# Moving GpSimd's share of the feed-forward stages of a hybrid encoder trunk onto VectorE

## The chip, the core and the metric

The kernel runs on one core of a Trainium2 chip. The metric is the device time of one execution in microseconds; the median of three runs of the kernel before is 2620.11 us (2618.71 to 2625.42). TensorE is called PE in the profile (PEld is its weight load), VectorE DVE, ScalarE ACT, GpSimd POOL, and SP is the engine whose queue issues most DMAs. L1043 is line 1043 of the kernel.

## The reference, cut to what matters

Two layers run on 1040 rows (16 learned rows ahead of 1024 tokens) of width 1024, all in float32. Each layer is a mixer (delta-rule heads and a short gated convolution, with its input and output projections) and then a feed-forward block:

```
h = h + hybrid_mixer(rmsnorm(h, norm1_w[l]), ...) # ends in mix @ w_out
h = h + swiglu(rmsnorm(h, norm2_w[l]), w_gate_up[l], w_down[l])

def swiglu(h, w_gate_up, w_down):
    gate, up = jnp.split(h @ w_gate_up, 2, axis=-1)     # each 2816 wide = 22 tiles of 128
    return (jax.nn.silu(gate) * up) @ w_down
```

A last RMSNorm ends it. The change touches the second line of each layer, and the output projection that runs into it.

## The kernel before, in words

**Split products.** Every matrix product is made of three passes in a fast float32 format. A weight tile w is split into a high part `hi` (ScalarE copies w into the format, which rounds it) and a low part `lo = w - hi`; the activations are split likewise. TensorE then adds `hi*hi + hi*lo + lo*hi`. So each weight tile that arrives by DMA costs one ScalarE copy and one subtraction before its matmuls, and the subtraction is what this case is about. Five places make such weights or work beside them in the feed-forward stages:

- `wsplit` (L123 to L130), called by `wload` (L132) for ordinary projections. Its subtraction at L130 goes to VectorE where the flag `lov[0]` is true and to GpSimd otherwise. `lov[0]` is set by position in the mixer (L642 and L748); from the third mixer tile of the second loop on it is false, and it is set again at the start of the next layer (L642).
- `w_op` (L1038 to L1044), the weights of the gate and up products: copy at L1042, subtraction at L1043 on GpSimd. It writes into a ring of seven pairs of slots (`wslot`, L1028).
- `w_unit` (L1163 to L1182), the weights of the down product: copy at L1180, subtraction at L1181 on GpSimd.
- L1330, the scaling of the gate row `g` by the inverse norm `ss`, on GpSimd; L1331 scales the row `u` on VectorE, then ScalarE applies SiLU (L1332), VectorE multiplies (L1333), and the row goes to memory by DMA (L1334).
- L950 in `out_part`, the sum of squares of the new residual. It is on VectorE except for the even tiles of the second half (z = 1), which GpSimd adds.

**Stages of the feed-forward part, in order, in each layer.** *Output projection with norm*: `out_part(z, m)` finishes the mixer's output projection for each of eight row tiles m in two halves of the columns z, adds it to the residual (L905 on VectorE, reading PSUM), sums squares, and between those calls VectorE and ScalarE form the combinations B11, B21, T1, B22, T2, T3, T4 of the normed activations, high and low (L177, L965, L977, L1001). *Early gate/up*: two of seven products of the first four tiles. *Gate/up*: for each of 22 tiles f, four quarter weights arrive by DMA, VectorE forms four combinations (L1266, L1267, L1270, L1271), seven weights go through `w_op`, and seven products (Strassen's scheme with seven instead of eight) run on TensorE. Each product lands in a PSUM bank and is taken out by VectorE (L1289, L1300, L1303, L1307, L1316) or ScalarE (L1285, L1312) before the next product adds into the same bank: p5 is followed by p3 in one bank, p6 by p7 by p4 in another. In layer 1 a product is two groups (j = 0, 1) of 12 matmuls of 260 columns; in layer 2 one group of 12 of 512 columns. *Down*: 18 of the 22 tiles go through the same seven-product scheme in 84 units; `w_unit(u)` makes weights five units ahead, `t_pair(t)` reloads the gate/up results from memory and splits them (L1222 on ScalarE, L1223 on VectorE) into eight slots; results are taken out at L1406. The four remaining tiles are an ordinary product with `wload` (layer 1) or `last_weights` (layer 2, L1360). Layer 2 ends in the final RMSNorm, where L1425 alternates between VectorE and GpSimd.

**What sets the order.** Each engine runs its own instructions strictly in the order of its queue, and waits on semaphores for the others. The order is not written by hand: the framework takes instructions in order of a priority (program order, moved by `at_prio`) as a planned timeline makes them ready, and fixes one order for each engine when the kernel is built. So an instruction that changes its engine may shift the order of its neighbours.

Of the kernel before, what the change touches and what calls it, by code (L numbers as in the profile page):

```python
# [7 lines left out]
F32 = mybir.dt.float32  # L8
# [3 lines left out]
ALU = mybir.AluOpType  # L12
# [30 lines left out]
def trunk(ctx: ExitStack, tc: tile.TileContext, xT, w_in, w_ba, w_out, w_gu, w_dn,  # L43
# [8 lines left out]
    def nm(p):  # L52
        cnt[0] += 1
        return f"{p}_{cnt[0]}"
# [4 lines left out]
    def row(tag, dt=F32, bufs=1):  # L59
        return sb.tile([128, L], dt, tag=tag, bufs=bufs, name=nm(tag))  # L60
# [4 lines left out]
    def c4k(tag="c"):  # L65
        return sb.tile([128, L], F32, tag="c", bufs=2, name=nm(tag))
# [28 lines left out]
    def at_prio(p):  # L95
        tc.cur_priority = p
# [3 lines left out]
    tt = nc.vector.tensor_tensor  # L100
    stt = nc.vector.scalar_tensor_tensor
    ts = nc.vector.tensor_scalar
    ptt = nc.gpsimd.tensor_tensor
# [17 lines left out]
    lov = [False]  # L121
# [23 lines left out]
    def dense(ws, xs, chunks, evac, pool=None):  # L145

        for (n0, n1) in chunks:
            n = n1 - n0
            ps = (pool or pacc)()
            K = len(xs)  # L150
            here = tc.cur_priority
            if mmp[0] is not None:
                at_prio(mmp[0])
            for k in range(K):
                (wh, wl), (xh, xl) = ws[k], xs[k]
                mm(ps[:, :n], wh, xh[:, n0:n1], start=(k == 0), stop=False)  # L156
                mm(ps[:, :n], wh, xl[:, n0:n1], start=False, stop=False)  # L157
                mm(ps[:, :n], wl, xh[:, n0:n1], start=False, stop=(k == K - 1))  # L158
            if mmp[0] is not None:
                mmp[0] = tc.cur_priority  # L160
                at_prio(here)
            here = tc.cur_priority
            if evp[0] is not None:
                at_prio(evp[0])
            evac(ps[:, :n], n0, n1)
            if evp[0] is not None:
                evp[0] = tc.cur_priority
                at_prio(here)
            for q in (jobs, jobs2, jobs3):
                f = q.pop(0) if q else None  # L170
                if f is not None:
                    f()
# [106 lines left out]
    for l in range(DEPTH):  # L279
# [656 lines left out]
            return v[:, s, :] if len(ap.shape) == 2 else v[:, :, s, :]  # L936

        at_prio(base + 3000000)
        ss = row("rstd")

        def out_part(z, m):
            dense(wload(w_out[l, m, :, 0:4, :], 4), os_, hcut[z], add_h(m), pwide)

            v, sv = half(hr[m][:, o0:L], z), half(ss[:, o0:L], z)
            if m == 0:
                act(out=sv, in_=v, func=AF.Square)
            else:
                sq = c4k("sq")[:, 0:NB].rearrange("p (g e) -> p g e", g=2)
                act(out=sq, in_=v, func=AF.Square)
                (ptt if z == 1 and m % 2 == 0 else tt)(out=sv, in0=sv, in1=sq, op=ALU.add)  # L950
            for (n0, n1) in hcut[z]:
                dma(hd[m][:, n0:n1], hr[m][:, n0:n1])

# [84 lines left out]
        def w_op(src, early=False):  # L1038
            hi, lo = wslot(early)
            n = src.shape[1]  # L1040
            hi, lo = hi[:, 0:n, :], lo[:, 0:n, :]
            act(out=hi, in_=src, func=AF.Copy)  # L1042
            ptt(out=lo, in0=src, in1=hi.bitcast(F32), op=ALU.subtract)  # L1043
            return hi, lo  # L1044

        bn = [0]
# [32 lines left out]
        def pin(ps):  # L1079
            return loc(ps, 0)  # L1080
# [82 lines left out]
        def w_unit(u):  # L1163

            p, b, m = UNITS[u]
            n = 4 * b + m
            i = u % 8
            if i in (0, 4, 6):
                hi, lo = (wp.tile([128, WK, 128], F32R, tag=t, name=nm(t)).rearrange("p a b -> p (a b)")[:, 0:384] for t in ("whi", "wlo"))
            else:  # L1170
                j = {1: 0, 2: 1, 3: 2, 5: 3, 7: 4}[i]
                hi, lo = (dw["W"][:, 384 * (2 * j + q):384 * (2 * j + q) + 384] for q in range(2))
            if p in ("P5", "P6", "P7"):
                r = s_raw(n)
            elif p == "P3":
                r = a_raw(0, 1, n)
                tt(out=r, in0=r, in1=s_raw(n), op=ALU.subtract)
            else:
                r = a_raw(*{"P2": (0, 1), "P1": (0, 0), "P4": (1, 1)}[p], n)
            act(out=hi, in_=r, func=AF.Copy)  # L1180
            ptt(out=lo, in0=r, in1=hi.bitcast(F32), op=ALU.subtract)  # L1181
            dw["w", u] = [t.rearrange("p (k e) -> p k e", k=3) for t in (hi, lo)]  # L1182

        def t_raw(i):
# [71 lines left out]
        for f in range(FT):  # L1256
            A11, A12, A21, A22 = raw4("raw"), raw4("raw"), raw4("ck2"), raw4("ck2")
            dma(A11, w_gu[l, f, 0, :, 0:4, :])
            dma(A21, w_gu[l, f, 1, :, 0:4, :])
            dma(A22, w_gu[l, f, 1, :, 4:8, :])  # L1260
            dma(A12, w_gu[l, f, 0, :, 4:8, :])
            s1t, s2t = raw4("ck2"), raw4("ck2")
            W = {}
            if f >= NE:
                W["A11"] = w_op(A11)
            tt(out=s1t, in0=A21, in1=A22, op=ALU.add)  # L1266
            tt(out=s2t, in0=s1t, in1=A11, op=ALU.subtract)  # L1267
            W["S1"] = w_op(s1t)
            W["S2"] = w_op(s2t)
            tt(out=s2t, in0=A12, in1=s2t, op=ALU.subtract)  # L1270
            tt(out=A21, in0=A11, in1=A21, op=ALU.subtract)  # L1271
            end = f == FT - 1
            for n, a in ([("S3", A21), ("A22", A22), ("S4", s2t), ("A12", A12)] if end else
                         [("S4", s2t), ("S3", A21), ("A12", A12), ("A22", A22)]):
                if f >= NE or n != "A12":
                    W[n] = w_op(a)
            g, u = early[f] if f < NE else (row((X[1], Y[1])[f % 2] + "f"), row(X[1], F32, 3))
            ps = {}


            def p1(j):
                ps["a", j], ps["c", j], ps["b", j] = pbank(), pbank(), pbank()
                if f >= NE:
                    prod(ps["a", j], W["A11"], T["B11"], j, True)
                    act(out=part(u, 0, j), in_=pin(ps["a", j]), func=AF.Copy)  # L1285

            def p5(j):
                prod(ps["c", j], W["S1"], T["T1"], j, True)
                tt(out=part(u, 1, j), in0=pin(ps["c", j]), in1=part(u, 0, j), op=ALU.add)  # L1289

            def p3(j):
                prod(ps["c", j], W["S4"], T["B22"], j, False)
                (gadd if end else gset)(ps["c", j], j)

            def p6(j):
                prod(ps["b", j], W["S2"], T["T2"], j, True)
                (gset if end else gadd)(ps["b", j], j)

            def gset(p, j):
                tt(out=part(g, 1, j), in0=pin(p), in1=part(u, 0, j), op=ALU.add)  # L1300

            def gadd(p, j):
                tt(out=part(g, 1, j), in0=pin(p), in1=part(g, 1, j), op=ALU.add)  # L1303

            def p7(j):
                prod(ps["b", j], W["S3"], T["T3"], j, False)
                tt(out=part(u, 1, j), in0=pin(ps["b", j]), in1=part(u, 1, j), op=ALU.add)  # L1307

            def p2(j):
                if f >= NE:  # L1310
                    prod(ps["a", j], W["A12"], T["B21"], j, False)
                    act(out=part(g, 0, j), in_=pin(ps["a", j]), func=AF.Copy)  # L1312

            def p4(j):
                prod(ps["b", j], W["A22"], T["T4"], j, False)
                tt(out=part(u, 0, j), in0=pin(ps["b", j]), in1=part(u, 0, j), op=ALU.add)  # L1316

            p1_ = (p1, p6, p7)
            if end:

                for p in (p1, p5, p6, p7, p4, p3, p2):
                    for j in range(NJ):
                        p(j)
                    down_begins(p)
            else:
                for j in range(NJ):
                    for p in (p1, p5, p3, p6, p7, p2, p4):
                        p(j)
            gv, uv, rv = g[:, o0:L], u[:, o0:L], ss[:, o0:L]
            ptt(out=gv, in0=gv, in1=rv, op=ALU.mult)  # L1330
            tt(out=uv, in0=uv, in1=rv, op=ALU.mult)  # L1331
            act(out=gv, in_=gv, func=AF.Silu)  # L1332
            tt(out=uv, in0=uv, in1=gv, op=ALU.mult)  # L1333
            dma(ad[f][:, o0:L], uv)  # L1334
            if NF <= f < NF + NP:
                tt(out=gv[:, 0:NB].rearrange("p (g e) -> p g e", g=2), in0=half(uv, 1), in1=half(uv, 0), op=ALU.subtract)
                dma(td[f - NF], gv[:, 0:NB])
            s_under(f)
# [38 lines left out]
        for u, (p, b, m) in enumerate(UNITS):  # L1377
            if b == 1 and p in FIRST:
                dh, z = FIRST[p]
# [13 lines left out]
            for j in range(NJ):  # L1393
# [9 lines left out]
                if b == NBK - 1:  # L1403
                    dh, z, op = TO[p]
# [98 lines left out]
```

## Time and profile before

| what | value |
|---|---|
| median of the three timed runs | 2620.11 us |
| span of the profiled execution, first to last instruction | 2625.6 us |
| mean granted TensorE clock in it | 0.983 |
| PE busy | 2512.3 us, 17442 matmuls |
| DVE busy | 1650.8 us, 2481 instructions |
| ACT busy | 1046.0 us, 1933 instructions |
| POOL busy | 1105.2 us, 838 instructions |

The profile shows one execution; no time of its own beside its span is given, and the span is 5.5 us above the median of the timed runs. A busy time counts from the start to the end of each instruction, so time in which a started instruction is held up counts as busy. A wait is listed as the waiting engine and line, an arrow, and the instruction that came last before it could go on. Idle time of an engine that is not the bottleneck costs nothing.

### The profile page before, as it was taken

The page shows a single profiled execution, that of the slowest core. Times are in us where ns is not written, and L with a number is a line of the kernel's source. Part 1 is how long each engine was busy: PE and PEld are TensorE (multiplying, and loading weights), DVE is VectorE, ACT ScalarE, POOL GpSimd, SP SyncE. Part 2 cuts the span into 40 slices and gives each one's busy share as a digit, 9 for nine tenths or more (in the row PEclk, how much of TensorE's full clock was granted, in tenths as well). Part 3 has the DMA queues.
Part 4 walks back from the last instruction along what each step waited for, and adds up shares of the span by engine and source line. Part 5 has one row for each costly group of instructions (what it writes and reads, how often), then busy time and mean ns, then how long its engine had stood idle before and what let it go on. Part 6 is the DMA issues. An engine that isn't in the chain of part 4 may idle for free. (4 is left out here: it accounts for less than half of the span.)

```text
span 2625.6 us, 45152 instructions
## 1 busy us (share of the span) xinstructions
PE 2512.3 (96%) x17442; PEld 2292.3 (87%) x17442; DVE 1650.8 (63%) x2481; ACT 1046.0 (40%) x1933; POOL 1105.2 (42%) x838
## 2 busy tenths in 40 slices
PE   8999999998999999989999989999989999998997
PEld 6989999998899999989999878998967778886876
DVE  4678433648766666667656874235688777668656
ACT  5564332435233333434445633324442323333444
POOL 2041212225666666645321212222357666665552
PEclk9999999999999999989999989999999999999999
DMA  3458265524422222763224572545333232248431
GB/s 125 127 179 267 88 196 171 183 66 126 136 97 86 102 81 74 242 203 113 94 88 140 177 249 92 184 157 197 111 128 125 91 108 85 76 140 274 130 111 64
DMA packets 213571, 360.03 MB, mean 137 GB/s; under 512 B 25268, under 2 KB 87676, under 8 KB 213356
## 3 DMA queue, kind: packets, MB, share of 16 engines
q1 hardware_dynamic: 180684, 310.69, 36.1%
q10 hardware_dynamic: 30496, 42.09, 5.1%
q0 software_dynamic: 2176, 4.36, 0.6%
q8 instruction: 137, 2.24, 0.4%
q14 instruction: 78, 0.64, 0.1%
HBM read 266.60 MB, written 90.46 MB: 136 GB/s over the span
## 5 line engine op out<-in xcount | busy, mean ns | idle before, releaser
L130 POOL TENSOR_TENSOR wlo<-raw,whi 128x512 fp32r<-128x512 f32 x132 | 178.3, 1353 | 802.7 <-ACT whi L129 723.0
L156 PE MATMUL pacc<-a,whi 128*128 128x346 f32 (+1 forms) x808 | 265.3, 332 | 11.9 <-ACT whi L129 10.4
L158 PE MATMUL pacc<-a,wlo 128*128 128x346 f32 (+1 forms) x808 | 264.7, 329 | 1.4 <-DVE wlo L130 0.7
L156 PE MATMUL pacc<-b,whi 128*128 128x346 f32 (+2 forms) x672 | 235.7, 351 | 0.4 <-DVE a L730 0.4
L158 PE MATMUL pacc<-b,wlo 128*128 128x346 f32 (+2 forms) x672 | 232.7, 348 | 0.0
L157 PE MATMUL pacc<-a,whi 128*128 128x346 f32 (+1 forms) x688 | 226.9, 330 | 2.6 <-DVE a L900 2.4
L157 PE MATMUL pacc<-b,whi 128*128 128x346 f32 (+2 forms) x580 | 201.2, 347 | 0.4 <-DVE b L900 0.4
L129 ACT ACTIVATE whi<-raw 128x512 fp32r<-128x512 f32 x168 | 105.0, 628 | 240.4 <-PE pacc L157 174.5
L156 PEld LDWEIGHTS pacc<-a,whi 128*128 128x128 f32 x808 | 154.0, 191 | 18.1 <-ACT whi L129 11.5
L1043 POOL TENSOR_TENSOR wlo<-rw,whi 128x512 fp32r<-128x512 f32 x92 | 134.7, 1466 | 72.2 <-ACT whi L1042 70.6
L158 PEld LDWEIGHTS pacc<-a,wlo 128*128 128x128 f32 x808 | 154.2, 191 | 3.3 <-issue 1.5
L157 PEld LDWEIGHTS pacc<-a,whi 128*128 128x128 f32 x688 | 132.0, 192 | 6.1 <-issue 2.7
L156 PEld LDWEIGHTS pacc<-b,whi 128*128 128x128 f32 x672 | 127.2, 189 | 10.8 <-issue 2.3
L158 PEld LDWEIGHTS pacc<-b,wlo 128*128 128x128 f32 x672 | 127.1, 189 | 9.8 <-issue 1.1
L1043 POOL TENSOR_TENSOR a<-rw,a 128x512 fp32r<-128x512 f32 x64 | 104.2, 1629 | 67.8 <-ACT a L1042 67.6
L1043 POOL TENSOR_TENSOR b<-rw,b 128x512 fp32r<-128x512 f32 x64 | 92.0, 1439 | 85.0 <-ACT b L1042 50.9
L157 PEld LDWEIGHTS pacc<-b,whi 128*128 128x128 f32 x580 | 109.8, 189 | 8.2 <-issue 0.8
L1042 ACT ACTIVATE whi<-rw 128x512 fp32r<-128x512 f32 x92 | 57.8, 630 | 144.3 <-DVE rw L1270 84.8
L1271 DVE TENSOR_TENSOR rw<-raw,rw 128x512 f32<-128x512 f32 x44 | 96.2, 2187 | 1.2
L1266 DVE TENSOR_TENSOR rw<-rw,rw 128x512 f32<-128x512 f32 x44 | 66.4, 1510 | 48.1 <-POOL wlo L1043 34.6
L1043 POOL TENSOR_TENSOR wlo<-raw,whi 128x512 fp32r<-128x512 f32 x50 | 77.9, 1562 | 34.3 <-ACT whi L1042 33.2
L1042 ACT ACTIVATE b<-rw 128x512 fp32r<-128x512 f32 x64 | 40.3, 630 | 122.0 <-PE pacc L1061 35.2
(970 smaller groups left out, 8417.8 us busy)
## 6 DMA issues: line engine op xcount, KB each, us to landing
raw<-in_w_in SPq DMA_DIRECT2D x112, 256.0 KB
raw<-in_w_gu SPq DMA_DIRECT2D x104, 256.0 KB
rw<-in_w_gu SPq DMA_DIRECT2D x88, 256.0 KB
rec<-aqd SPq DMA_DIRECT2D x62, 256.0 KB
rec<-vkd SPq DMA_DIRECT2D x61, 256.0 KB
rw<-in_w_dn SPq DMA_DIRECT2D x70, 192.0 KB
raw<-in_w_out SPq DMA_DIRECT2D x48, 256.0 KB
b<-ad SPq DMA_DIRECT2D x45, 260.0 KB
```

Source lines behind the costliest of these rows:

```text
L129: act(out=hi, in_=raw[:, 0:kk, :], func=AF.Copy)
L130: (tt if lov[0] else ptt)(out=lo, in0=raw[:, 0:kk, :], in1=hi.bitcast(F32), op=ALU.subtract)
L156: mm(ps[:, :n], wh, xh[:, n0:n1], start=(k == 0), stop=False)
L157: mm(ps[:, :n], wh, xl[:, n0:n1], start=False, stop=False)
L158: mm(ps[:, :n], wl, xh[:, n0:n1], start=False, stop=(k == K - 1))
L1042: act(out=hi, in_=src, func=AF.Copy)
L1043: ptt(out=lo, in0=src, in1=hi.bitcast(F32), op=ALU.subtract)
L1266: tt(out=s1t, in0=A21, in1=A22, op=ALU.add)
L1271: tt(out=A21, in0=A11, in1=A21, op=ALU.subtract)
```

## The change

`lov[0]` becomes true where the output projection with norm begins, and so stays for all `wsplit` calls up to the next layer's first projection; the other four places call VectorE's `tt` in place of GpSimd's `ptt`. No operand, tile or DMA is changed.

```diff
         at_prio(base + 3000000)
+        lov[0] = True
         ss = row("rstd")
...
                 act(out=sq, in_=v, func=AF.Square)
-                (ptt if z == 1 and m % 2 == 0 else tt)(out=sv, in0=sv, in1=sq, op=ALU.add)
+                tt(out=sv, in0=sv, in1=sq, op=ALU.add)
...
             act(out=hi, in_=src, func=AF.Copy)
-            ptt(out=lo, in0=src, in1=hi.bitcast(F32), op=ALU.subtract)
+            tt(out=lo, in0=src, in1=hi.bitcast(F32), op=ALU.subtract)
             return hi, lo
...
             act(out=hi, in_=r, func=AF.Copy)
-            ptt(out=lo, in0=r, in1=hi.bitcast(F32), op=ALU.subtract)
+            tt(out=lo, in0=r, in1=hi.bitcast(F32), op=ALU.subtract)
             dw["w", u] = [t.rearrange("p (k e) -> p k e", k=3) for t in (hi, lo)]
...
             gv, uv, rv = g[:, o0:L], u[:, o0:L], ss[:, o0:L]
-            ptt(out=gv, in0=gv, in1=rv, op=ALU.mult)
+            tt(out=gv, in0=gv, in1=rv, op=ALU.mult)
             tt(out=uv, in0=uv, in1=rv, op=ALU.mult)
```

In numbers of instructions, over both layers: 308 at L1043 (154 in a layer: 8 early, 5 for each of four tiles, 7 for each of 18), 168 at L1181 (84 units in a layer), 44 at L1330, 6 at L950 and 48 at L130 (16 in `out_part` and 8 for the last four tiles, in each layer). GpSimd keeps what it has in the mixer and its half of L1425.

## The prediction

> **What bounds the kernel now.** I read the busy times first, then a table by stage, then what PE waited for in the feed-forward stages, then the moments of those waits.
>
> ```profile
> PE 2512.3 (96%) x17442; PEld 2292.3 (87%) x17442; DVE 1650.8 (63%) x2481; ACT 1046.0 (40%) x1933; POOL 1105.2 (42%) x838
> ```
>
> PE does all the time it can; no other engine is near full. The change moves no matmul, so it can only change the 113 us in which PE is not busy, and of these only what falls in the feed-forward stages. The table by stage has PE, PEld, DVE, ACT and POOL busy, then the granted clock, the DMA share and GB/s:
>
> ```profile
> core 0: us, PE busy (x) PEld busy (x) DVE busy (x) ACT busy (x) POOL busy (x), PEclk, DMA share, GB/s
> ...
> 580.00:650.00 70.00, 63.11 (x504) 61.93 (x503) 60.27 (x81) 38.98 (x65) 34.28 (x23) 0.98 0.46 137
> 650.00:1080.00 430.00, 417.38 (x3435) 412.32 (x3434) 276.43 (x359) 142.51 (x250) 275.17 (x170) 1.00 0.29 96
> 1080.00:1275.00 195.00, 185.09 (x1525) 184.88 (x1524) 136.78 (x194) 81.28 (x149) 103.46 (x84) 0.96 0.58 187
> ...
> 1893.00:1950.00 57.00, 49.17 (x298) 41.79 (x297) 49.92 (x59) 29.02 (x46) 28.47 (x19) 0.97 0.38 123
> 1950.00:2345.00 395.00, 387.40 (x1661) 312.12 (x1660) 283.32 (x246) 126.60 (x200) 272.23 (x164) 1.00 0.30 100
> 2345.00:2545.00 200.00, 188.20 (x789) 150.45 (x788) 140.17 (x169) 86.98 (x159) 105.95 (x89) 0.97 0.60 191
> 2545.00:2626.00 81.00, 63.04 (x361) 54.18 (x359) 43.13 (x64) 30.47 (x59) 23.77 (x21) 0.92 0.17 59
> ```
>
> The rows are the output projection with norm, gate/up and down of layer 1, the same three of layer 2, and the tail. PE's idle time in them is length less busy: 6.9, 12.6, 9.9, 7.8, 7.6, 11.8 and 18.0 us. That is 75 us, the whole stake. The tail's 18 is the final norm and the last output, which the change hardly touches, so 56.6 us remain. What PE waited for, stage by stage (total, times, longest):
>
> ```profile
> PE pacc L1060 <- DVE a L905: 2.5, 1, 2.5
> ...
> PE pa L1062 <- POOL wlo L1043: 0.6, 1, 0.6
> ...
> PE pacc L1060 <- DVE a L1307: 5.6, 11, 1.5
> PE pb L1060 <- DVE a L1307: 2.5, 4, 1.3
> ...
> PE pf L1400 <- ACT P L1222: 9.9, 1, 9.9
> ...
> PE pf L156 <- DVE b L905: 2.1, 1, 2.1
> PE pb L1062 <- POOL wlo L1043: 1.6, 2, 1.2
> PE pacc L1062 <- POOL wlo L1043: 1.2, 1, 1.2
> ...
> PE pf L1060 <- DVE b L1307: 3.4, 3, 2.0
> ...
> PE pb L1400 <- DVE b L1406: 7.5, 1, 7.5
> ```
>
> Two things are to be seen. Only 3.4 us (0.6, 1.6, 1.2) are waits for a low part that GpSimd makes. In gate/up PE waits in many small pieces for VectorE to take a product out of its bank (L1307), although VectorE is busy for only 276 of 430 us there. One such piece in order of time (start, length, engine, line):
>
> ```profile
> 802.24 2.90 POOL L1330 TENSOR_TENSOR b3f<-b3f,rstd 128x1040 f32<-128x1040 f32 x1
> ...
> 802.87 2.81 DVE L1271 TENSOR_TENSOR rw<-raw,rw 128x512 f32<-128x512 f32 x1
> ...
> 805.60 0.41 DVE L1307 TENSOR_TENSOR a<-pacc,a 128x260 f32<-128x260 f32 x1
> ...
> 806.07 0.39 PE L1060 MATMUL pacc<-a,a 128*128 128x260 f32 x1 [0.40 <-DVE a L1307]
> ```
>
> L1271 starts while GpSimd's L1330 runs and ends half a microsecond after it, at 805.68; the take-out L1307 comes behind it, and PE stands for 0.40 us. How long L1271 is when nothing is in its way, and what the moved operations cost on VectorE, is in the rows of single lines (nanoseconds, least/median/most):
>
> ```profile
> L1271 DVE TENSOR_TENSOR rw<-raw,rw x44: 674/2784/2827, 650.9 to 2326.8; 128x512 f32<-128x512 f32 x44
> L130 DVE TENSOR_TENSOR wlo<-raw,whi x36: 665/683/710, 83.0 to 1535.2; 128x512 fp32r<-128x512 f32 x36
> L1331 DVE TENSOR_TENSOR a<-a,rstd x21: 1227/1244/2062, 681.9 to 1092.0; 128x1040 f32<-128x1040 f32 x21
> L1150 DVE TENSOR_TENSOR b<-a,b x4: 543/558/1181, 1196.0 to 1206.8; 128x384 f32<-128x384 f32 x4
> L1307 DVE TENSOR_TENSOR a<-pacc,a x15: 414/416/429, 693.1 to 1087.3; 128x260 f32<-128x260 f32 x15
> ```
>
> A VectorE operation with two inputs in SBUF takes 674 ns at best and 2784 in the median; one that reads PSUM (L1307) never varies. So the first kind is held up by GpSimd's running instruction, to its end, and the time counts as busy.
>
> **The change, part by part.** *Added on VectorE.* The 308 subtractions of L1043 and 48 of L130 are 128x512 at 0.683 us: 243 us. The 168 of L1181 are 128x384 at 0.558: 94. The 44 of L1330 are as large as L1331, at 1.244: 55. The six of L950, of the size of L130's, 4. Together 574 instructions and 396 us; VectorE then has 3055 instructions, GpSimd 264.
>
> *Removed from VectorE.* The time held up goes. In gate/up of layer 1 the groups were:
>
> ```profile
> L1271 DVE TENSOR_TENSOR rw<-raw,rw 128x512 f32<-128x512 f32 x22 | 47.2, 2144 | 0.5
> L1266 DVE TENSOR_TENSOR rw<-rw,rw 128x512 f32<-128x512 f32 x21 | 34.0, 1617 | 31.2 <-POOL wlo L1043 28.2 <-DMA rw<-in_w_gu 3.0
> ...
> L1267 DVE TENSOR_TENSOR rw<-rw,raw 128x512 f32<-128x512 f32 x22 | 18.2, 827 | 9.3 <-POOL a L1043 9.2
> L1270 DVE TENSOR_TENSOR rw<-raw,rw 128x512 f32<-128x512 f32 x22 | 18.1, 821 | 1.8 <-POOL a L1043 1.7
> L1333 DVE TENSOR_TENSOR a<-a,a3f 128x1040 f32<-128x1040 f32 x9 | 15.7, 1746 | 0.0
> ```
>
> At 0.674 each, L1271, L1266, L1267 and L1270 would be 58.6 us in place of 117.5; 20 of L1333 at 1.23 in place of 1.75 give another 10. So 69 us go, 0.25 us for each of GpSimd's 275 busy microseconds. I use this quarter as an estimate for the other stages.
>
> *Load by stage.* Gate/up of layer 1 gets 146 subtractions and 21 scalings, 126 us: 276 - 69 + 126 = 333 of 430 us, 77% in place of 64%. Layer 2 is alike: 283 - 68 + 126 = 341 of 395, 86%, an upper end since its L1271 group is held up longer. Output projection: layer 1 has 23 instructions moved at 0.683, 15.7 us, less a quarter of 34.3: 60.3 + 15.7 - 8.6 = 67.4 of 70. Layer 2, 19 moved: 49.9 + 13.0 - 7.1 = 55.8 of 57. Down: 84 units, 47 us, less 26: 158 of 195 and 161 of 200. VectorE stays below the stage's length everywhere, though barely in the output projection.
>
> *Gate/up, what it is worth.* The time of an instruction ahead of a take-out falls from up to 2.9 us to at most 1.24 (L1330 and its like), mostly 0.68; but there are more of them. A layer 1 product is 12 matmuls of 417.38/3435 = 0.1215 us, 1.46 us in all; PE runs on through another product while a take-out of 0.42 us is made, so some 1.0 us of lateness is free. A 2.8 us hold-up exceeds it, a 0.68 does not, a 1.24 just does. Bounds: all 12.6 and 7.6 us of PE's idle time go, or none does and the fuller queue adds as much again. I take half, 6.3 and 3.8, nearer to the rows since the only pieces above 1.0 that remain are the 22 scalings and L1331, L1333 of each layer.
>
> *Output projection.* The 3.4 us of waiting for GpSimd's low parts go, since the same subtraction ends in half the time. But VectorE is nearly full from end to end, and the take-outs L905 (2.5 and 2.1 us above) come later when the queue backs up. In layer 1 the added 15.7 exceed the relief by 7.1; 9.7 us were unused, so the end is between nothing and 7 us later. I take 2 us back: net -1.4.
>
> *The two stalls of down.* The 9.9 us of layer 1 end when a reload lands; there VectorE and DMA look like this, and so does layer 2's 7.5 us:
>
> ```profile
> 1110.00:1120.00 10.00, 6.25 (x53) 6.03 (x51) 7.73 (x11) 3.09 (x6) 1.53 (x2) 0.92 1.08 362
> 1120.00:1130.00 10.00, 3.84 (x17) 3.84 (x18) 3.65 (x7) 1.28 (x3) 0.39 (x1) 0.50 0.77 257
> ...
> 2405.00:2415.00 10.00, 10.00 (x45) 7.96 (x44) 10.00 (x14) 4.79 (x10) 7.61 (x7) 1.00 0.52 158
> 2415.00:2425.00 10.00, 4.25 (x19) 3.09 (x17) 10.00 (x14) 3.22 (x7) 5.23 (x5) 0.86 0.52 156
> ```
>
> The first is a transfer limit (DMA share 1.08) with VectorE idle a fifth of the time: nothing changes. The second is VectorE full for 20 us with the take-out L1406 at the end of its queue. Twelve moved subtractions add 6.7 us there; a quarter of POOL's 12.8 gives 3.2 back. Bounds: 7.5 saved, or 3.5 added; I take nothing.
>
> *The rest.* The DMAs wait for the low parts to free raw tiles, and these come sooner, never later than now unless VectorE's queue is late; the eight subtractions in the tail stand beside matmuls. Sum: -6.3 - 3.8 - 1.4 = -11.5 us. Against the span of 2625.6 that is 2614.1; the span stands 5.5 above the median of the timed runs, and against the median it is 2608.6, say **2609 us**.
>
> A rule speaks against it: the Trainium skill, Perfetto Trace Analysis, section Optimizing Scalar/DVE Operations, says that work may be handed to Scalar or GpSimd when DVE is saturated, and adds that between GpSimd and DVE this may not help because they share a read port. By its first half the output projection, where the trace has DVE at 60.27 of 70 us, should lose by the change; by its second half it should not, and the 2784 against 674 ns of L1271 bear the second half out. The first half's result is the second rival below.
>
> **The rivals.** *One, slower: the queue stands still behind a subtraction.* A low part on VectorE waits for ScalarE's high part, which waits for PE to free the slot. GpSimd stood waiting for these in layer 1's gate/up (microseconds, times):
>
> ```profile
>   ACT a L1042: 109.4, 58
>   ACT whi L1042: 41.0, 24
> ```
>
> That is 1.83 us each time, and it cost nothing because nothing else was in that queue. On VectorE a take-out may be queued behind. If it is, PE loses 1.83 less the 1.0 that is free, 0.8 us. With one in ten of the 308 subtractions so placed it is 25 us and no gain: 2645; it decides from one in twenty (12 us), where it eats the gain. For it speaks that the order is fixed when the kernel is built; against it, that a plan places the subtraction after the copy, and that PE's own lateness moves both. *Two, no change:* VectorE's load, not its hold-ups, makes the take-outs late. Then gate/up gains nothing, and the output projections, with 15.7 and 13.0 us put on 60.3 and 49.9 without relief, are 6 us longer each, less the 3.4: about 2620 to 2629, 2622 as the point with half of that. For it speak 67.4 of 70 us; against it the timeline at 802. *Three, faster by more:* the stall at 2415 goes as well, with its half-speed matmuls behind it (clock 0.50 in the row at 1120 shows what follows a stall), and so do nearly all gate/up pieces: 12.6 + 7.6 + 7.5 less 1 for the rest, 27 us, 2593. That the change doesn't do what it says is ruled out by L642, which sets the flag anew in each layer; only the order could surprise.
>
> **How the numbers follow.** Forecast 0.38 (2609, own range 2600 to 2612), rival three 0.07, rival two 0.25, rival one 0.30. A difference under 0.3%, 7.9 us, can't be told from none here; so faster is 0.38 + 0.07 = 0.45, same 0.25, slower 0.30. For 8 in 10 the range reaches from rival three's 2593 to rival one's 2645, leaving out half of each.
>
> **What would show it.** POOL busy falls to about a quarter; VectorE has 3055 instructions and, with a quarter of the seven rows' 844 us of POOL taken off and 396 added, some 1,836 us; L1271's median falls to 0.68 us and L1266's to the like. PE's waits for L1307 fall to half or less: if they stay and L1271 is short, rival two holds; if DVE waits for ACT L1042 show up ahead of L1043 and PE's waits for take-outs grow, rival one. The waits for POOL L1043 must be gone. The prediction is wrong if PE's idle time in gate/up does not fall by some 10 us in all, or if a stall over 5 us appears in the output projection.

## The result

The changed kernel takes 2572.69 us in the median (2565.86 to 2574.73, 4 runs), the kernel before 2619.75 on the same chip; the ratio is 0.9821, with a 95% interval of 0.9804 to 0.9839. It is 47 us faster, where the prediction had 11 (2609 against 2620) and a range down to 2593. The sign was right, the size wrong by a factor of four. In the profiled executions the spans are 2625.6 and 2572.3 us, 53.3 apart; the comparison below is between these two. The first is 5.9 us above the median of its timed runs and the second 0.4 below, so some 6 of the 53.3 us are not the change's, and which stage holds them is not known. Lines behind L938 stand one further down than before: L1043 is now L1044.

The first line of the changed kernel's profile:

```profile
PE 2493.8 (97%) x17442; PEld 2285.1 (89%) x17442; DVE 1722.1 (67%) x3055; ACT 1046.3 (41%) x1933; POOL 246.3 (10%) x264
```

The instruction counts are as predicted, 3055 and 264. VectorE is busier by only 71 us although 574 instructions of 396 us were added: 1650.8 + 396 - 1722.1 = 325 us are gone from the busy time. Not all of that is time in which VectorE stood. An instruction often starts some 0.08 us before the one ahead of it has ended, and the busy time counts this overlap once; with more instructions there is more of it. Added up by instruction, VectorE's durations are 1757.2 us before and 1877.6 after, of which the moved ones take 394.6; so the old instructions got 274 us shorter, and that is the standing that went. The table by stage, for about the same pieces of the program as before (columns as before; the windows end earlier since the stages are shorter):

```profile
core 0: us, PE busy (x) PEld busy (x) DVE busy (x) ACT busy (x) POOL busy (x), PEclk, DMA share, GB/s
...
580.00:650.00 70.00, 65.36 (x530) 64.92 (x530) 64.78 (x110) 43.29 (x73) 0.00 (x0) 0.98 0.48 144
650.00:1060.00 410.00, 410.00 (x3419) 409.32 (x3418) 312.13 (x526) 137.66 (x245) 0.00 (x0) 1.00 0.31 101
1060.00:1265.00 205.00, 194.94 (x1615) 194.73 (x1614) 150.69 (x285) 83.69 (x153) 0.00 (x0) 0.98 0.56 180
...
1870.00:1920.00 50.00, 45.85 (x290) 39.03 (x289) 47.79 (x80) 30.84 (x48) 0.00 (x0) 1.00 0.42 138
1920.00:2305.00 385.00, 384.74 (x1661) 311.37 (x1660) 285.29 (x406) 126.36 (x197) 0.00 (x0) 1.00 0.29 101
2305.00:2492.00 187.00, 184.61 (x792) 148.20 (x791) 150.04 (x259) 87.33 (x160) 0.00 (x0) 1.00 0.64 205
```

In these two gate/up windows (the second row and the fifth) PE has almost no idle time left: 410.00 of 410 and 384.74 of 385. What PE still waits for between 560 and 1300 us, and then the longest waits of the whole execution:

```profile
PE pf L1401 <- ACT P L1223: 10.1, 1, 10.1
PE pb L1063 <- DVE wlo L1044: 2.5, 1, 2.5
PE pf L1061 <- ACT whi L1043: 2.1, 1, 2.1
```

```profile
PE pf L1401 <- ACT P L1223: 10.1, 1, 10.1
PE pacc L156 <- ACT whi L129: 9.6, 3, 5.9
PE pb L489 <- DVE dt L499: 7.9, 3, 5.2
PE pa L196 <- DVE rstd L188: 5.4, 1, 5.4
```

Not one wait for a take-out (VectorE or ScalarE reading a product out of its bank) is left in layer 1's gate/up. What is left there are two waits for a weight at its start, one of them 2.5 us for a low part that VectorE now makes. The transfer-limited stall at the start of down is there unchanged (9.9, now 10.1), and the rest of the list lies in the mixers and in the final norm. The rows of the instructions behind it, L1271 (now L1272) and one of the moved subtractions:

```profile
L1272 DVE TENSOR_TENSOR rw<-raw,rw x44: 679/682/693, 648.5 to 2287.8; 128x512 f32<-128x512 f32 x44
...
L1044 DVE TENSOR_TENSOR wlo<-rw,whi x92: 678/683/694, 647.3 to 2303.9; 128x512 fp32r<-128x512 f32 x92
```

The median of L1271 fell from 2784 to 682 ns and the spread is gone: with GpSimd silent, this instruction takes the same time each time.

To compare stages of equal work I cut both traces at the same instructions: the mixer up to its last transpose (L871), "out" up to the first matmul of L1060, "gate/up" from there up to the first of L1400 (it holds the second half of the output projection too), "down" up to the next layer's first matmul (in layer 2 up to the last matmul of L1400), and the rest. Lengths in us, PE's idle time in brackets:

| kernel | mixer 1 | out 1 | gate/up 1 | down 1 | mixer 2 | out 2 | gate/up 2 | down 2 | rest |
|---|---|---|---|---|---|---|---|---|---|
| before | 547.7 | 75.4 (2.0) | 470.0 (17.5) | 193.7 (9.9) | 582.0 | 52.3 (3.0) | 441.1 (12.4) | 197.3 (11.8) | 66.0 |
| after | 549.0 | 72.9 (0.0) | 451.4 (4.6) | 193.0 (10.1) | 578.9 | 47.4 (0.0) | 429.7 (4.4) | 183.9 (2.4) | 66.0 |
| difference | +1.3 | -2.5 | -18.6 | -0.7 | -3.1 | -4.9 | -11.4 | -13.4 | 0.0 |

Gate/up gave 30.0 us, layer 2's down 13.4, the output projections 7.4. The mixers, in which nothing changed, moved between 545 and 552 and between 574 and 585 us over the profiles of this study (save one, told below), so differences of a few microseconds in any one section can be of that kind.

### The profile page after: what moved, and what is told of

Read it like the earlier page. It is cut to its first block, busy times and chain, and to the rows that moved or that the text cites. A ratio compares the mean times of both kernels' runs of the same rounds, so it can differ in the third digit from the quotient of the medians.

```text
span 2572.3 us, 44715 instructions
## 1 busy us (share of the span) xinstructions
PE 2493.8 (97%) x17442; PEld 2285.1 (89%) x17442; DVE 1722.1 (67%) x3055; ACT 1046.3 (41%) x1933; POOL 246.3 (10%) x264
## 4 chain that ended last, share of the span: by engine, by line
PE 76%; DVE 9%; DMA 8%; issue 2%; ACT 2%; POOL 1%; ACTq 0%; SPq 0%; POOLq 0%; DVEq 0%
PE pacc L156 7%; PE pacc L158 7%; PE pacc L157 7%; PE pacc L1063 4%; PE pacc L1061 4%; PE pacc L1062 4%; PE pb L1063 3%; PE pb L1061 3%; PE pb L1062 3%; PE pf L1061 3%; PE pf L1063 3%; PE pf L1062 3%; PE pacc L1401 2%; PE pacc L1403 2%; PE pacc L1402 2%
## 5 line engine op out<-in xcount | busy, mean ns | idle before, releaser
L130 POOL TENSOR_TENSOR wlo<-raw,whi 128x512 fp32r<-128x512 f32 x92 | 123.1, 1340 | 1427.3 <-ACT whi L129 1357.1
L156 PEld LDWEIGHTS pacc<-a,whi 128*128 128x128 f32 x808 | 154.6, 192 | 19.8 <-ACT whi L129 10.7
L1043 ACT ACTIVATE whi<-rw 128x512 fp32r<-128x512 f32 x92 | 58.1, 631 | 128.6 <-DVE rw L1271 29.8
L1043 ACT ACTIVATE b<-rw 128x512 fp32r<-128x512 f32 x64 | 40.2, 632 | 143.7 <-PE pacc L1062 47.3
L295 DVE TENSOR_TENSOR a<-pacc,rstd 128x346 f32<-128x346 f32 (+2 forms) x59 | 32.6, 553 | 83.7 <-PE pacc L158 83.6
L1426 POOL TENSOR_TENSOR b<-b,rstd 128x256 f32<-128x256 f32 (+1 forms) x12 | 13.3, 1137 | 726.2 <-DVE rstd L198 726.2
L1043 ACT ACTIVATE a<-rw 128x512 fp32r<-128x512 f32 x64 | 40.2, 629 | 101.6 <-PE pacc L1062 72.2
L295 DVE TENSOR_TENSOR b<-pacc,rstd 128x346 f32<-128x346 f32 (+1 forms) x63 | 32.2, 512 | 70.8 <-PE pacc L158 70.7
L1044 DVE TENSOR_TENSOR wlo<-rw,whi 128x512 fp32r<-128x512 f32 x92 | 62.9, 685 | 6.3 <-ACT whi L1043 5.6
L130 DVE TENSOR_TENSOR wlo<-raw,whi 128x512 fp32r<-128x512 f32 x76 | 52.3, 688 | 15.8 <-ACT whi L129 15.2
```

The lines of the kernel that those rows point to most:

```text
L130: (tt if lov[0] else ptt)(out=lo, in0=raw[:, 0:kk, :], in1=hi.bitcast(F32), op=ALU.subtract)
L295: tt(out=t[:, n0:n1], in0=ps, in1=rstd[:, n0:n1], op=ALU.mult)
```

## The experiments

**Which part gives what.** Four kernels, each the one before with one part of the change; the edits are these (each alone, in the same order as the labels p1 to p4):

```diff
-            ptt(out=lo, in0=src, in1=hi.bitcast(F32), op=ALU.subtract)   # L1043
+            tt(out=lo, in0=src, in1=hi.bitcast(F32), op=ALU.subtract)
...
-            ptt(out=gv, in0=gv, in1=rv, op=ALU.mult)                     # L1330
+            tt(out=gv, in0=gv, in1=rv, op=ALU.mult)
...
-            ptt(out=lo, in0=r, in1=hi.bitcast(F32), op=ALU.subtract)     # L1181
+            tt(out=lo, in0=r, in1=hi.bitcast(F32), op=ALU.subtract)
...
+        lov[0] = True                                                    # L130, and L950
-                (ptt if z == 1 and m % 2 == 0 else tt)(out=sv, in0=sv, in1=sq, op=ALU.add)
+                tt(out=sv, in0=sv, in1=sq, op=ALU.add)
```

> The kernel before with only the 308 gate/up subtractions moved to VectorE; the scaling of the gate row, the down weights and the projection stay on GpSimd. Hold-up theory (VectorE operations with two SBUF inputs stand while a GpSimd instruction runs, and the take-outs behind them come late): gate/up loses the hold-ups of L1266, L1267 and L1270 but keeps that of L1271 by the 2.9 us scaling, whose median stays near 2.8 us; some 18 us less than before, about 2602 us, and nothing gained in down. Order theory (the gain is the new order of PE's and VectorE's instructions, which any change of engine shuffles): a change of anywhere between 15 us less and 15 us more, also in stages that have no moved instruction.

> The kernel before with only the 44 scalings of the gate row moved. Hold-up theory: L1271's median falls from 2.8 to about 1.3 us, PE's waits for L1307 fall by half, about 10 us less than before, 2610 us. Order theory: anywhere within 15 us of before.

> The kernel before with only the 168 subtractions of the down weights moved. Hold-up theory: the stall of 7.5 us in layer 2's down product, where VectorE is full, shrinks to 3 us or less, the 9.9 us one in layer 1 stays; about 12 us less than before, 2608 us, and gate/up as before. Order theory: anywhere within 15 us of before, gate/up changed too.

> The kernel before with only the 48 projection subtractions and the 6 sums of squares moved. Hold-up theory: the output projections of both layers gain 3 us each, about 6 us less than before, 2614 us. My prediction's step (a nearly full VectorE queue backs up): between 1 us less and 6 us more. Order theory: anywhere within 15 us.

Measured against 2618.29 us of the kernel before on that chip (the pair in the last row, which was run later, against 2620.61). The stages are differences of the one profiled execution from that of the kernel before; for p1 and p3 it was a long one, 13 and 12 us above the median of the same kernel, so their stages are uncertain by some microseconds:

| part | median us | ratio (95% interval) | out 1 | gate/up 1 | down 1 | out 2 | gate/up 2 | down 2 |
|---|---|---|---|---|---|---|---|---|
| p1, L1043 | 2585.20 | 0.9872 (0.9840 to 0.9903) | -1.0 | -15.6 | +2.4 | -1.2 | -9.9 | -6.5 |
| p2, L1330 | 2602.40 | 0.9926 (0.9906 to 0.9946) | +0.2 | -12.2 | +0.9 | -1.2 | -1.9 | -3.5 |
| p3, L1181 | 2614.20 | 0.9985 (0.9969 to 1.0002) | +0.1 | 0.0 | +0.6 | -1.5 | +0.9 | -8.9 |
| p4, L130 and L950 | 2606.92 | 0.9950 (0.9928 to 0.9973) | -2.5 | -1.5 | +1.4 | -4.9 | -0.3 | -6.3 |
| p1 and p2 together | 2581.94 | 0.9858 (0.9841 to 0.9875) | -1.9 | -19.8 | +1.7 | -2.2 | -13.0 | -10.3 |

By the totals I had expected 2602, 2610, 2608 and 2614 us: p1, p2 and p4 gained more than that, p3 less, and p3's interval holds 1, so alone it is not told from no change. In the main the stages answer to the part that is in them: p4 gives out 1 and out 2 the whole of the change's -2.5 and -4.9, p3 leaves both gate/up stages alone, p1 and p2 give gate/up and leave layer 1's down alone. That speaks against a gain that is only a luckier order, which would have moved stages at random. The exception is layer 2's down, which gained in all four, told below. And the parts don't add up: 33.1, 15.9, 4.1 and 11.4 us make 64, where all together give 47. One thing I expected of p1 did not come. With GpSimd's scaling left in place, L1271 should have stayed held up at 2.8 us; its row (L1272 in these kernels), for p1 and then for p4, where gate/up is untouched:

```profile
L1272 DVE TENSOR_TENSOR rw<-raw,rw x44: 675/685/2944, 653.9 to 2306.7; 128x512 f32<-128x512 f32 x44
```

```profile
L1272 DVE TENSOR_TENSOR rw<-raw,rw x44: 675/2780/2809, 644.9 to 2311.9; 128x512 f32<-128x512 f32 x44
```

In p1, 14 of the 44 are still held up, 30 are not: with the subtractions in VectorE's queue the two instructions mostly no longer come at the same moment. So who is held up does depend on the order, and p1 and p2 can each remove the same hold-up, which would explain why their gains overlap. In p2, which moves only the scalings, the row falls further than the 1.3 us that I expected:

```profile
L1272 DVE TENSOR_TENSOR rw<-raw,rw x44: 676/678/1789, 650.8 to 2307.0; 128x512 f32<-128x512 f32 x44
```

This hold-up can be counted in the kernel before. From 785 to 1056 us PE waits 13 times for L1307, 0.40 to 0.42 us each time, and ahead of each of these take-outs an L1271 has stood for 2.1 us; these are 13 of the 26 stalls of layer 1's gate/up. p2, in which L1271 is free, has 12.2 us of that stage's 18.6.

In layer 2's down the order can't be excluded. The stall of 7.5 us behind a full VectorE queue stays at 7.5 us in p2 and 6.8 in p4, is 4.9 in p1, and is gone only in p3, which moves the subtractions of that stage (PE waits 3.1 us for one of these low parts there). But p4, which has nothing moved there before the stage's end, still has -6.3: the second stall of the stage (3.2 us) is gone, and PE spends 6.8 us at a granted clock of 0.5 in place of 13.6. Which part is owed how much there is left open.

The pair together was run later, to see whether gate/up by itself goes as in the full change:

> The kernel before with the 308 gate/up subtractions and the 44 scalings moved; down and projection stay on GpSimd. Hold-up theory, stage by stage: gate/up as in the changed kernel (451 and 430 us against 470 and 441 before), the output projections as in the run with the subtractions alone, down still 190 us or more in layer 2; 2585 us. Order theory: gate/up differs from the changed kernel by more than 5 us.

It does, within 2 us in each layer; down in layer 2 fell to 187.0 us without any of its own subtractions moved, against the "190 us or more" expected. Against its own comparison of 2620.61 it is 38.7 us faster.

**Hold-up or order: the same order with GpSimd at work again.** The next kernels are the changed one, with work on GpSimd that nothing waits for. Each piece starts behind a ScalarE copy of a weight (or behind the up side's scaling on VectorE, L1331 before and L1332 now) and touches only a spare tile. The built order of PE's, VectorE's and ScalarE's instructions is that of the changed kernel (in e_echo3 with 15 matmuls and two VectorE instructions in other places); on the SP queue the load of one small constant of layer 2 comes later, since the spare tile is that constant's place. The edit of e_echo; e_half has half as many additions, e_echo3 half as many again, and e_quiet has memsets of the same tiles in their place:

```diff
-            act(out=hi, in_=src, func=AF.Copy)
+            ah = act(out=hi, in_=src, func=AF.Copy)
             tt(out=lo, in0=src, in1=hi.bitcast(F32), op=ALU.subtract)
+            for q in range(2):
+                after(ptt(out=sc1[:, 0:256], in0=sc1[:, 0:256], in1=sc1[:, 0:256], op=ALU.add), ah if q == 0 else None)
...
+            for q in range(2):                        # the same behind the down copies, 192 columns
+                after(ptt(out=sc1[:, 0:192], in0=sc1[:, 0:192], in1=sc1[:, 0:192], op=ALU.add), ah if q == 0 else None)
...
-            tt(out=uv, in0=uv, in1=rv, op=ALU.mult)  # L1332
+            ah = tt(out=uv, in0=uv, in1=rv, op=ALU.mult)
+            for q in range(4):
+                after(ptt(out=sc1[:, 0:256], in0=sc1[:, 0:256], in1=sc1[:, 0:256], op=ALU.add), ah if q == 0 else None)
```

> The changed kernel with idle GpSimd work added that nobody reads or waits for: behind each copy of a gate/up weight two memsets of a spare tile (128x256), behind each of a down weight two (128x192), behind each scaling four. The order of PE, VectorE and ScalarE is that of the changed kernel. Memsets read nothing. Hold-up theory: if only GpSimd instructions that read SBUF stand in VectorE's way, 2573 us within 5; if any does, as the run that adds a tile to itself. Order theory: 2573 us within 5.

> The changed kernel with half of the idle work, and of the reading kind: one addition of the spare tile to itself (128x256, or 128x192 in down) behind each weight copy and two behind each scaling; order of PE, VectorE and ScalarE unchanged. Hold-up theory: VectorE's operations of two SBUF inputs lengthen again, some 8 us more than the changed kernel, 2581 us. Order theory: 2573 us within 5.

> As the one before with two additions behind each weight copy and four behind each scaling: about the GpSimd time that the change took away from gate/up and down, though in pieces of 256 columns, so no single hold-up is as long as the 2.9 us scaling was. Order unchanged. Hold-up theory: L1266's and L1271's medians (one line further down) rise from 0.68 us to 1 us or more, VectorE's busy time by 100 us or more, and some 20 us of the 47 are lost again, 2593 us. Order theory: 2573 us within 5.

> Half as much again: three additions behind each weight copy, six behind each scaling; the order of PE differs in 15 matmuls, VectorE's in two instructions. Hold-up theory: about 30 us of the 47 lost, 2603 us or more. Order theory: 2573 us within 5.

Measured: e_quiet 2571.35 us, e_half 2584.66, e_echo 2632.33, e_echo3 2804.24; the kernel before 2620.26 on that chip, where the changed kernel was not run again. Of e_half and e_echo I had expected 2581 and 2593; the loss was larger both times. The order theory expected 2573 of all four and falls: with the order of the fast kernel and GpSimd's additions back, the time is above that of the kernel before (ratio 1.0043, 1.0027 to 1.0060). The first lines of the pages of e_half, then e_echo:

```profile
PE 2504.3 (97%) x17442; PEld 2293.1 (89%) x17442; DVE 1828.0 (71%) x3055; ACT 1046.0 (40%) x1933; POOL 778.5 (30%) x830
```

```profile
PE 2514.9 (96%) x17442; PEld 2297.9 (87%) x17442; DVE 1955.6 (74%) x3055; ACT 1043.4 (40%) x1933; POOL 1276.2 (48%) x1394
```

The same 3055 VectorE instructions are busy for 1722.1, 1828.0 and 1955.6 us. So 106 and 234 us of standing cost 12 and 60 us of the whole (against 2572.69). The cost grows faster than its cause, I take it because VectorE runs full; e_echo by stage, in windows from the cuts of the table:

```profile
617.00:1078.00 461.00, 450.80 (x3715) 447.86 (x3715) 411.20 (x582) 161.41 (x289) 365.76 (x385) 0.99 0.32 106
1078.00:1281.00 203.00, 186.42 (x1509) 185.13 (x1508) 179.06 (x268) 77.24 (x143) 133.83 (x177) 0.96 0.51 160
1910.00:2353.00 443.00, 430.24 (x1837) 345.38 (x1836) 406.39 (x467) 151.76 (x241) 372.71 (x367) 0.99 0.31 106
2353.00:2565.00 212.00, 188.52 (x777) 149.47 (x777) 194.28 (x249) 80.54 (x150) 151.52 (x195) 0.95 0.52 161
```

VectorE is busy for 89% and 92% of gate/up and 88% and 92% of down. Against the changed kernel gate/up is longer by 8.5 and 12.9 us and down by 10.7 and 28.5. So e_echo is not the change undone: the change gained most in gate/up, e_echo loses most in down, and layer 1's gate/up stays 10 us shorter than in the kernel before. PE's waits are in part others too, for low parts that VectorE makes now (L1047 and L1187 here); two each of the longest in layer 1's gate/up behind 640 us and in layer 2's down:

```profile
PE pa L1068 <- DVE wlo L1047: 1.8, 2, 1.6
PE pacc L1066 <- DVE a L1324: 1.2, 1, 1.2
...
PE pacc L1412 <- DVE a L1187: 8.8, 1, 8.8
PE pb L1410 <- DVE b L1416: 5.8, 1, 5.8
```

What e_echo shows is that VectorE's standing by itself, in one and the same order, costs PE this much; that it cost layer 1's gate/up the whole 18.6 us rests mainly on the count above and on p2. L1271 (here L1279) is held up only as long as one short addition lasts:

```profile
L1279 DVE TENSOR_TENSOR rw<-raw,rw x44: 677/1096/1101, 648.0 to 2321.1; 128x512 f32<-128x512 f32 x44
```

e_echo3 shows something else than I meant it to. Of the 168 us that its span has over e_echo's, 43 lie in the second mixer (624.3 against 581.4) and 81 in the last section (147.3 against 66.2), where GpSimd has work of its own that comes late behind the added queue (in the second mixer PE waits 40 us once for a low part of L130); down is 18 us longer in each layer, and gate/up only 7 and 1. It is no third point on the same line.

**Is it the reading?** e_quiet's memsets are short (POOL was busy for 333 us with them, 1030 with e_echo's additions), so a kernel with three times as many was run:

> The changed kernel with three times the idle memsets: six of 128x256 behind each gate/up copy, six of 128x192 behind each down copy, twelve behind each scaling, about as much GpSimd time (1,000 us) as the additions that gave 2632 us, and again the same order of PE, VectorE and ScalarE. Hold-up by reading instructions: 2573 us within 5. Hold-up by any GpSimd work, or by its waits and semaphores: 2600 us or more.

```profile
PE 2496.7 (97%) x17442; PEld 2287.5 (89%) x17442; DVE 1724.5 (67%) x3055; ACT 1047.4 (41%) x1933; POOL 1249.0 (48%) x3650
```

```profile
L1279 DVE TENSOR_TENSOR rw<-raw,rw x44: 680/686/694, 646.1 to 2289.1; 128x512 f32<-128x512 f32 x44
```

With as much GpSimd time as in e_echo, VectorE's busy time is that of the changed kernel within 2.4 us, and gate/up (450.2, 430.4) and down (193.0, 183.9) too. The total is 2580.78 us, 8 above the changed kernel, where 5 at most were expected: 5.7 of it is the final norm (71.7 against 66.0), where GpSimd's half comes late behind the memsets. So it is neither GpSimd's being busy nor its semaphores that holds VectorE, but instructions that read SBUF, here with two inputs. This is as the Trainium skill has it (SBUF — State Buffer, section SBUF: two separate sides): a VectorE instruction with two SBUF inputs and a GpSimd instruction that reads SBUF exclude each other for a whole instruction. A memset writes SBUF too, so GpSimd's writing alone holds nothing here.

**Further the same way.** Two kernels take more off GpSimd: f1 the last 92 weight subtractions of the projections, f2 also L679, L726, L739, L742, the GpSimd case of L900 and of the final norm's scaling:

```diff
-        (tt if lov[0] else ptt)(out=lo, in0=raw[:, 0:kk, :], in1=hi.bitcast(F32), op=ALU.subtract)
+        tt(out=lo, in0=raw[:, 0:kk, :], in1=hi.bitcast(F32), op=ALU.subtract)
...
-            ptt(out=t0, in0=t0, in1=rstd, op=ALU.mult)        # f2, and its like
+            tt(out=t0, in0=t0, in1=rstd, op=ALU.mult)
```

> The changed kernel with the remaining 92 weight subtractions of the projections moved to VectorE too. Hold-up theory: VectorE is half idle in the mixers and PE waits there mostly for other things, so little is to be had: 5 us less, 2568 us. Order theory: anywhere within 10 us of 2573.

> As the one before, and the mixer's scalings and products, one low part of the gated convolution and the half of the final norm's scaling moved as well; GpSimd keeps only two small inversions of 4 rows and its DMAs. Hold-up theory: another 3 us less, 2565 us; the final norm's end, where VectorE and GpSimd share the last four rows, loses 2 us. Order theory: anywhere within 10 us of 2573.

f1 takes 2566.86 us (ratio to before 0.9798, 0.9779 to 0.9817), which is not told from the changed kernel's 0.9804 to 0.9839; f2 takes 2557.19 (0.9754, 0.9732 to 0.9775), which is 15 us faster than the changed kernel and the fastest here. The first line of its page stands below. I expected 2565 of f2 and a loss in the final norm; the rest took 62.6 us in place of 66.0, and out 1 63.4 in place of 72.9.

```profile
PE 2490.6 (97%) x17442; PEld 2283.3 (89%) x17442; DVE 1773.4 (69%) x3185; ACT 1047.1 (41%) x1933; POOL 57.6 (2%) x134
```

## Why the prediction was right in sign and wrong in size

**What held.** The mechanism: VectorE's two-input operations stood while GpSimd ran, take-outs came late, PE waited. The added work (396 us, 574 instructions), PE's waits for GpSimd's low parts (gone), the transfer-limited stall of layer 1 (unchanged), and L1271's fall to 0.68 us all came as said. So did the sign, though the forecast had given faster only 0.45.

**The step that failed first: "I take half, 6.3 and 3.8".** Gate/up gave 18.6 and 11.4 us. I bounded the gain by PE's listed idle time and then halved it. Nearly all of it went (17.5 to 4.6 and 12.4 to 4.4 in the sections of the table): scalings and products of 1.22 to 1.25 us are still in VectorE's queue, and PE's waits for VectorE's take-outs are gone, all but one of 0.3 us in layer 2. The argument with 1.0 us of free lateness put the border too low. And the bound was not one. A stall costs PE more than is listed as idle: the neighbours of the stalled matmul at 806.07 that the prediction shows, the one ahead of it and the one behind it, are

```profile
805.39 0.28 PE L1062 MATMUL pb<-P,a 128*128 128x260 f32 x1
...
806.30 0.28 PE L1061 MATMUL pacc<-a,a 128*128 128x260 f32 x1
```

From start to start the three are 0.68 and 0.23 us apart, where the matmuls around it have 0.12: 0.67 us lost, 0.40 listed. The same count over all stalls of layer 1's gate/up (the distances to the matmul ahead and the one behind, less the median distance of 0.120 us) gives 24.3 us lost for 17.5 listed in 26 stalls before, and 5.2 for 4.6 in two stalls after; the difference is 19.1 us, where the stage gained 18.6. In layer 2 (median distance 0.232 us) it went from 15.7 us in 14 stalls to 6.3 in seven, 9.4 of the 11.4.

**The relief of VectorE, "a quarter" of GpSimd's time.** 274 us of standing went with 1105.2 - 246.3 = 859 us of GpSimd's work, 0.32 for each. I had read it from five groups of layer 1's gate/up, 69 us; with the smaller groups it is 84 there, and in layer 2's gate/up, for which I took 68, it is 109. That is 63 us more than the quarter gives, and the larger overlap takes another 49 off the busy time. So VectorE's load was put too high: 1,836 us against 1722.1, and 86% in layer 2's gate/up against 285.29/385, 74% (77% in layer 1 was right: 312.13/410, 76%).

**The output projection, "net -1.4".** I took VectorE's queue for nearly full and gave 2 us back for it; measured -2.5 and -4.9 in the cuts of the table, by these parts alone (p4). A busy share of 60.27 in 70 that holds time spent standing was no measure of how full VectorE was; and being full did not make its take-outs late: it is busy for 64.78 of the 70 us now, and PE's idle time in the section went from 2.0 us to nothing. That it was the standing that made them late follows by the other stages; no run separates the two here. The rule of the Trainium skill that I weighed there (Perfetto Trace Analysis, section Optimizing Scalar/DVE Operations: handing work from a saturated DVE to GpSimd) did not apply: VectorE took on 15.7 us and the stage got shorter.

**Layer 2's down, "I take nothing".** The stage gave 13.4 us, beyond my bound of 7.5 for the one stall, since the second one and the half-speed matmuls after both went too: the granted clock in the last row of the stage table is 1.00 in place of 0.97. The second stall before, and what is left after:

```profile
PE pa L1400 <- DVE b L1406: 3.2, 1, 3.2
...
PE pacc L1403 <- DVE a L1182: 2.0, 1, 2.0
PE pb L1401 <- DVE b L1407: 0.4, 1, 0.4
```

I had put this stage at nothing because the added subtractions and the relief seemed to cancel; that the stall itself hung on GpSimd is shown only in part (p3 removes it, p4's gain there is unexplained).

**The rivals.** Rival one did not come: VectorE stood ahead of the subtractions for ScalarE (L1044), but briefly.

```profile
  ACT a L1043: 14.0, 27
  ACT b L1043: 12.1, 13
  ACT whi L1043: 6.1, 13
```

That is 32 us in 53 pieces of 0.6 us, where GpSimd had stood 1.83 us each time; I take it that the built order puts other work in between. Rival two (VectorE's load, not its hold-ups) falls by e_echo against the changed kernel: the same VectorE instructions in the same order, 60 us apart. Rival three, at 0.07, was nearest and still 20 us short.

## What to carry to other kernels

Read an engine's busy time against the least duration of the same instruction: if the median is far above it, the share of busy time holds waiting, and moving the other engine's work onto the "full" one can cost it far less than that work takes (here 71 us of busy time for 396 us of work). Bound what a stall costs by the distance between the starts of matmuls, not by the listed idle time. And to tell a hold-up from a luckier order, put idle work back on the engine in question in a kernel with the order unchanged, and look whether the same stages lose by the same waits.

## What the runs showed of the hardware that was not expected

The cost of the two engines' excluding each other grows faster than the standing: 106 us of standing cost 12 us, 234 cost 60. These are two points only; that a full VectorE is the reason is not shown. GpSimd's memsets and its additions differ by more than their length: some 1,000 us of memsets cost VectorE 2.4 us of busy time, some 1,030 us of additions 233.
